# A fixed order for the opening of a hybrid decoder step: small rows, constants and key norms moved

## The chip, the cores and the metric

The kernel runs on one core of a Trainium2 chip. The metric is the device time of one execution in microseconds (us): the median of several runs. Before the change it is 1969.95 us (three runs, 1969.76 to 1970.19).

The engines of a core run side by side, each through its own list of instructions in order, and wait for one another by semaphores: TensorE (PE: matrix products and transposes, into PSUM banks), VectorE (DVE), ScalarE (ACT), GpSimd (POOL), and SyncE (SP), which here only issues transfers (DMA).

## The reference, cut to what matters

One layer of a decoder, on a prompt of 2048 tokens and on 8 samples of one token each. All of it is float32, D_MODEL is 1024.

```python
mod = (c @ w_ada + b_ada)[:, None, :]
shift, scale, gate = jnp.split(mod, 3, axis=-1)
h = _rmsnorm(x, norm_g) * (1.0 + scale) + shift
z = h @ w_in
q, k, v, ga, xr, gr, ma, mr = jnp.split(z, offs, axis=-1)
q = _rmsnorm(q.reshape(B, T, N_HEADS, HEAD_DIM), q_g)
k = _rmsnorm(k.reshape(B, T, KV_HEADS, HEAD_DIM), k_g)
o = _band_attention(q, k, v, rel_table, sinks)      # window of 128, bias by distance
ya = o * jax.nn.silu(ga)
xc, conv_new = _causal_conv(xr, conv_buf, w_conv, b_conv)
hs, h_last = _rglru(xc, h0, w_ra, b_ra, w_rx, b_rx, lam)
yr = hs * jax.nn.silu(gr)
merged = jax.nn.sigmoid(ma) * (ya @ w_pa) + jax.nn.sigmoid(mr) * (yr @ w_pr)
y = x + gate * (merged @ w_out)
```

In the recurrent branch (_rglru) the decay is exp(-8 r softplus(-lam)) with r = sigmoid(x @ w_ra + b_ra). The constants of that branch are softplus(-lam) for each of the 1024 channels, worked out by a series, and half the biases of the two gates.

## The kernel before

The prompt is done in two halves of 1024 rows (s = 0, 1). A float32 product is made of three products of rounded parts: each operand is split into a high part (a cast on ACT) and a low part (source minus high, on DVE), and PE adds high x high, high x low and low x high. A weight's step thus waits first for ACT's cast and, at its third matmul, for DVE's split.

**The opening** (s = 0) is the loop over f = 0 to 9 near line 2053. Turn f loads w_ada columns, multiplies them by the vector c on PE (col_tiled, L295, whose result ACT copies to a tile H), transposes that tile on PE and reduces it on DVE (mod_finish, L310) to shift and scale of 128 channels (modT, gsT). PE turns a column block of the first four normed x tiles (x_turn), and ACT, then DVE, evacuate it as scaled high and low parts (h_evac, L376). Between these stand the matmuls of the first four tiles of keys and values (kv_part), two turns behind. rms_rows (x_rms) norms an x tile: squares on ACT, the power on POOL, the products on DVE. In turns 7 to 9 the other four x tiles are turned (second). This part is recorded with `pinned[0] = True`: the scheduler keeps the order in which it is written. Into it are set: in turn 4 the loads of the rows of small vectors (vrows_rest, nine transfers of 0.2 to 16 KB), in turns 5 and 6 the two steps of the table of biases (bias_table: a transpose, a copy on DVE, a matmul, a store to Ed), in turn 7 the loads from Ed.

**Then, not pinned,** come the transposes of the small rows to VT, the stores of h (late, sixteen of them), the constants of the recurrent branch (ba2, c4: two activations and 25 operations on 128 x 8 elements, L2107 to L2124), the states of the samples (rows, turned by eight small transposes on PE to RT), and the stage of keys and values (phase_kv, L502). There k_tile (L449) norms a tile's keys in two steps: the first takes the squares (ACT), sums them (DVE), takes the power (POOL) and multiplies (DVE), the second turns the keys on PE and evacuates them; v_tile copies the values and subtracts the tile before. The scheduler may mix these with the matmuls of the next tiles (half). phase_attn (L554) is a generator: at its first step it issues the first loads of weights, at the second it splits some.

PSUM's eight banks are shared: tag g has three, q two, t three. In the opening the first three key tiles hold the banks of g and the fourth one bank of t, so that turns, column sums, transposes and the table of biases go through two banks of t.

**After the attention** a list of steps runs (class Line): step t is twelve matmuls on PE, and then the events of step t in the order EVAC, SIDE, SPLIT, FORM, CHAIN, LATE, STORE, LOAD. The weights of a step are loaded seven steps and split two steps ahead. gate_side (SIDE, steps 10 to 39) makes the gate's columns.

Of the kernel before, what the change touches and what calls it, by code (L numbers as in the profile page):

```python
# [16 lines left out]
ALU = mybir.AluOpType  # L17
# [24 lines left out]
def tile_hybrid_step(ctx: ExitStack, tc: tile.TileContext, x_prompt, x_sample, cache_k, cache_v, state_conv,  # L42
# [63 lines left out]
    def H(shape, dt=F32):  # L106
        return hp.tile([P] + shape, dt, tag="H", name=nm("H"))
# [341 lines left out]
    def k_tile(s, tt, ps, kT):  # L449

        ss = head_rstd(ps, P)
        kn = H([4, HD])
        V.tensor_tensor(kn, ps[:, :256].rearrange("p (h d) -> p h d", d=HD),
                        ss.unsqueeze(2).broadcast_to([P, 4, HD]), op=ALU.mult)
        yield
        p2 = PT()
        for Gp in range(2):
            T_.transpose(p2[:, Gp * P:(Gp + 1) * P], kn[:, 2 * Gp:2 * Gp + 2, :].rearrange("p h d -> p (h d)"), ident)
        for Gp in range(2):
            src = p2[:, Gp * P:(Gp + 1) * P]  # L460
# [41 lines left out]
    def phase_kv(s, hT, sa, kT, vt, wk, wv, start, tts, side, attn):  # L502


        def half(ps, tt, h):
            for j, w in enumerate((wk, wv)):
                for k in range(4 * h, 4 * h + 4):
                    wh, wl, _ = w[k]
                    xh, xl = col(hT, k, tt * P, P)
                    o = ps[:, j * 256:(j + 1) * 256]  # L510
                    T_.matmul(o, xh, wh, start=(j == 0 and k == 0), stop=False, skip_group_check=True)
                    T_.matmul(o, xh, wl, start=False, stop=False, skip_group_check=True)
                    T_.matmul(o, xl, wh, start=False, stop=(k == KT - 1), skip_group_check=True)

        pend = []

        def evac(ps, tt):
            pend.append(k_tile(s, tt, ps, kT))
            next(pend[-1])
            v_tile(s, tt, ps[:, 256:512], vt)  # L520

        def flush(n):
            while len(pend) > n:
                next(pend.pop(0))

        next(attn)
        for tt, ps in start:
            evac(ps, tt)
        for tt in tts[:-2]:
            ps = PQ()  # L530
            half(ps, tt, 0)
            flush(1)
            half(ps, tt, 1)
            evac(ps, tt)
            next(side, None)
            next(side, None)
        if s == 1:
            kv_samples(wk, wv, sa)
        two = [(tt, PG()) for tt in tts[-2:]]
        for tt, ps in two:  # L540
            half(ps, tt, 0)
            flush(0)
            next(side, None)
        drop(wk[0:4] + wv[0:4])
        next(attn)
        for tt, ps in two:
            half(ps, tt, 1)
            evac(ps, tt)
        drop(wk[4:8] + wv[4:8])
        for _ in side:  # L550
            pass
        return pend

    def phase_attn(s, hT, sa, kT, vt, chunks, line):  # L554
# [257 lines left out]
        pinned[0] = True  # L812
# [440 lines left out]
    def stages(s, hT, hT1=None, side=None):  # L1253
# [603 lines left out]
    def reload_h(line, hT, k, c, t):  # L1857
# [11 lines left out]

        line.on(t - 3, LOAD, load)  # L1870
        line.on(t, FORM, split)

    def gate_side():

# [178 lines left out]
    for f in range(KT + 2):  # L2053
# [38 lines left out]
    ba2 = C([P, 16], tag="ba2")  # L2092
    V.tensor_scalar(ba2, VT[:, 72:88], 0.5, None, op0=ALU.mult)


    sk = M([NH])
    ld.dma_start(sk, sinks[0].partition_broadcast(P))
# [5 lines left out]

    kT, vt = kv_tiles()
    wk, wv = wkv[0][0] + wkv[1][0], wkv[0][1] + wkv[1][1]

    lam = VT[:, 88:96]  # L2107
    e8, s8, q8, r8 = (M([8]) for _ in range(4))
    A.activation(e8, lam, AF.Abs)
    A.activation(e8, e8, AF.Exp, scale=-1.0)  # L2110
    V.tensor_scalar(s8, e8, 2.0, None, op0=ALU.add)
    V.reciprocal(s8, s8)
    V.tensor_tensor(s8, s8, e8, op=ALU.mult)
    V.tensor_tensor(q8, s8, s8, op=ALU.mult)
    V.tensor_scalar(r8, q8, 1.0 / 17, 1.0 / 15, op0=ALU.mult, op1=ALU.add)
    for n in (13, 11, 9, 7, 5, 3, 1):
        V.tensor_tensor(r8, r8, q8, op=ALU.mult)
        V.tensor_scalar(r8, r8, 1.0 / n, None, op0=ALU.add)
    V.tensor_tensor(r8, r8, s8, op=ALU.mult)
    V.tensor_scalar(s8, lam, -1.0, 0.0, op0=ALU.mult, op1=ALU.max)  # L2120
    c4 = C([P, 16], tag="c4")
    V.scalar_tensor_tensor(c4[:, 0:8], r8, 2.0, s8, op0=ALU.mult, op1=ALU.add)
    V.tensor_scalar(c4[:, 0:8], c4[:, 0:8], 4.0, None, op0=ALU.mult)
    V.tensor_scalar(c4[:, 8:16], c4[:, 0:8], -1.0, None, op0=ALU.mult)  # L2124


    rows = S([D])
    ld.dma_start(rows[0:24], state_conv[0].rearrange("b r d -> (b r) d"))
    ld.dma_start(rows[24:32], state_h[0])
    ps = PT()  # L2130
    for k in range(KT):
        T_.transpose(ps[:, k * 32:(k + 1) * 32], rows[0:32, k * P:(k + 1) * P], ident[0:32, 0:32])
    RT = C([P, KT, 32], tag="RT")
    V.tensor_copy(RT, ps[:, 0:256].rearrange("p (k c) -> p k c", c=32))
    free(rows)
# [8 lines left out]
    line = stages(1, hT1)  # L2144
    kT, vt = kv_tiles()
    attn = phase_attn(1, hT1, side["sa"], kT, vt, chunks, line)
    pend = phase_kv(1, hT1, side["sa"], kT, vt, side["k"], side["v"], [], range(8), iter(()), attn)
    attn.send(pend)
    line.run()
# [28 lines left out]
```

## Time and profile before

| what | value |
|---|---|
| median of three runs | 1969.95 us |
| the profiled execution | 1970.57 us |
| its span, first to last instruction | 1968.9 us |
| mean granted clock of PE | 0.996 |
| PE busy | 1918.9 us, 97% |
| DMA | 286.61 MB, 146 GB/s |

A profile's timeline gives start, duration, engine, line, operation, the tile written and the tiles read, and in brackets how long the engine had been idle and what ended that. All tiles go through one helper, so that every line is L60, and operations are told apart by their tiles: S, B, H and M are SBUF tiles (rings of 28 and 35, and pools of 6 and 16), pg, pq and pt are PSUM banks of tags g, q and t. A window's row gives its bounds, its length, an engine's busy time, PE's granted clock (1.00 is full speed), the DMA engines' busy share and GB/s.

### The profile page before, as it was taken

The numbers are of one execution on the slowest core, as the hardware profiler recorded it, in microseconds if no ns is written. First come the engines' busy times: TensorE is split into PE (matmuls) and PEld (weight loads), VectorE is DVE, ScalarE is ACT, GpSimd is POOL, SyncE is SP. The second block draws the span as 40 slices with busy tenths as digits, with TensorE's granted clock in tenths as the row PEclk, the third lists the DMA queues.
The fourth block names the chain that finished last, engine by engine and source line by source line (L and its number), as shares of the span: only waits on it lengthen the run. The fifth ranks groups of instructions, "written<-read, shape, count | busy, mean of one in ns | idle before, by whom it ended". The sixth has DMA issues, their size and how long they took to land. (4 is left out here: it accounts for less than half of the span.)

```text
span 1968.9 us, 32371 instructions
## 1 busy us (share of the span) xinstructions
PE 1918.9 (97%) x11504; PEld 1569.0 (80%) x11504; DVE 1376.8 (70%) x2862; ACT 985.0 (50%) x2167; POOL 391.3 (20%) x476
## 2 busy tenths in 40 slices
PE   6899999999999999999999999999999999999999
PEld 4798986778888878877898888777887887777777
DVE  3557778567887876587735776776677879755965
ACT  4435665336575766323424555543475667532321
POOL 2213443000111113150022333300010201111600
PEclk9899999999999999999999999999999999999999
DMA  9521125652433567976611111544233325458673
GB/s 280 175 65 51 48 77 158 202 171 93 138 118 100 176 190 251 330 243 191 228 47 49 55 34 51 160 124 151 82 119 108 126 93 167 144 170 300 214 236 108
DMA packets 307686, 286.61 MB, mean 146 GB/s; under 512 B 57073, under 2 KB 224229, under 8 KB 307486
## 3 DMA queue, kind: packets, MB, share of 16 engines
q1 hardware_dynamic: 307398, 282.41, 45.8%
q0 software_dynamic: 128, 2.15, 0.3%
q8 instruction: 90, 1.47, 0.3%
q14 instruction: 70, 0.57, 0.1%
HBM read 200.69 MB, written 85.93 MB: 146 GB/s over the span
## 5 line engine op out<-in xcount | busy, mean ns | idle before, releaser
L60 PE MATMUL pg<-S,B 128*128 128x512 f32 (+1 forms) x4224 | 1003.7, 392 | 4.2 <-DVE B L60 3.8
L60 PEld LDWEIGHTS pg<-S,B 128*128 128x128 f32 (+1 forms) x4224 | 773.9, 188 | 188.6 <-issue 11.1
L60 DVE TENSOR_TENSOR B<-B,B 128x512 fp32r<-128x512 f32 (+1 forms) x732 | 540.9, 761 | 145.8 <-ACT B L60 136.0
L60 PE MATMUL pq<-S,B 128*128 128x512 f32 (+2 forms) x1920 | 412.2, 379 | 6.7 <-DVE B L60 6.6
L60 PEld LDWEIGHTS pq<-S,B 128*128 128x128 f32 (+1 forms) x1920 | 317.0, 188 | 85.2 <-DVE B L60 10.6
L60 POOL TENSOR_TENSOR B<-B,B 128x512 f32<-128x512 f32 x128 | 191.4, 1513 | 921.5 <-DVE B L60 363.5
L60 ACT CAST B<-B 128x512 fp32r<-128x512 f32 x468 | 279.9, 617 | 111.4 <-DVE B L60 71.5
L60 PE MATMUL pg<-B,S 128*128 128x256 f32 x1872 | 243.3, 286 | 0.0
L60 PEld LDWEIGHTS pg<-B,S 128*128 128x128 f32 x1872 | 228.1, 189 | 10.1 <-issue 9.4
L60 DVE TENSOR_TENSOR S<-B,S 128x512 fp32r<-128x512 f32 x184 | 144.6, 814 | 25.9 <-ACT S L60 25.7
L60 ACT CAST S<-B 128x512 fp32r<-128x512 f32 x184 | 109.3, 620 | 94.0 <-DVE B L60 40.7
L60 ACT ACTIVATE B<-B 128x512 f32<-128x512 f32 (+1 forms) x150 | 93.1, 629 | 117.0 <-DVE B L60 109.0
L60 ACT ACTIVATE B<-B,M 128x129 f32<-128x129 f32 x260 | 102.6, 396 | 91.3 <-DVE M L60 87.1
L60 DVE SCALAR_TENSOR_TENSOR B<-B,pg 128x512 f32<-128x512 f32 x78 | 53.1, 682 | 72.9 <-PE pg L60 63.1
L60 ACT COPY H<-pt 128x256 f32<-128x256 f32 (+1 forms) x55 | 18.5, 337 | 160.9 <-PE pt L60 160.9
L60 DVE TENSOR_TENSOR B<-pq,B 128x512 f32<-128x512 f32 x96 | 65.9, 686 | 44.3 <-PE pq L60 38.3
L60 POOL TENSOR_TENSOR B<-B,M 128x512 f32<-128x512 f32 x64 | 68.6, 1093 | 122.8 <-DVE M L60 122.8
L60 ACT COPY B<-pg 128x512 f32<-128x512 f32 x80 | 46.8, 586 | 89.4 <-PE pg L60 81.1
L60 ACT ACTIVATE B<-pg 128x512 f32<-128x512 f32 x76 | 45.2, 595 | 85.3 <-PE pg L60 85.3
L60 POOL TENSOR_TENSOR M<-M,mhalf 128x8 f32<-128x8 f32 (+4 forms) x70 | 83.8, 1198 | 5.8
L60 DVE SCALAR_TENSOR_TENSOR B<-B,VT,B 128x512 f32<-128x512 f32 x96 | 81.2, 846 | 2.3
L60 DVE TENSOR_TENSOR B<-pt,mcT 128x512 f32<-128x512 f32 x64 | 41.7, 686 | 47.4 <-ACT B L60 45.5
(201 smaller groups left out, 1718.6 us busy)
## 6 DMA issues: line engine op xcount, KB each, us to landing
B<-in_w_in_dram SPq DMA_DIRECT2D x144, 256.0 KB
B<-in_w_in_dram SPq DMA_DIRECT2D x128, 128.0 KB
B<-yad SPq DMA_DIRECT2D x56, 256.0 KB
B<-hd SPq DMA_DIRECT2D x48, 256.0 KB
B<-in_w_out_dram SPq DMA_DIRECT2D x48, 256.0 KB
S<-in_w_ada_dram SPq DMA_DIRECT2D x32, 256.0 KB
S<-in_x_prompt_dram SPq DMA_DIRECT2D x16, 512.0 KB
hd<-B SPq DMA_DIRECT2D x32, 256.0 KB
```

The source lines that it names most:

```text
L60: ins = fn(*args, **kw)
```

## The change

All of the opening and of the attention's first part is now recorded in the written order; the pieces that were left to the scheduler are put in places:

- The table of biases goes from turns 5 and 6 to turns 2 and 3; the loads of small rows go from turn 4 to turn 6, behind all loads of w_ada.
- The first eight stores of h are issued in turn 8, the other eight behind the first loads of the attention's weights.
- ba2, c4 and RT are made by a generator rnn_side in steps 16 (loads), 22 (constants) and 24 (transposes) of the list of steps of half 0.
- k_tile yields once more, between the power and the product, and evac takes several tiles: the first four are normed in two pairs, all later ones singly, with the values' copy and subtraction ahead of the product.

```diff
     def k_tile(s, tt, ps, kT):
 
         ss = head_rstd(ps, P)
+        yield
         kn = H([4, HD])
...
-        def evac(ps, tt):
-            pend.append(k_tile(s, tt, ps, kT))
-            next(pend[-1])
-            v_tile(s, tt, ps[:, 256:512], vt)
+        def evac(*tiles):
+            gens = [k_tile(s, tt, ps, kT) for tt, ps in tiles]
+            for g in gens:
+                next(g)
+            for tt, ps in tiles:
+                v_tile(s, tt, ps[:, 256:512], vt)
+            for g in gens:
+                next(g)
+            pend.extend(gens)
...
-        next(attn)
-        for tt, ps in start:
-            evac(ps, tt)
+        for n in range(0, len(start), 2):
+            evac(*start[n:n + 2])
...
         prefetch(3)
-        pinned[0] = s == 1
-        yield
-        pinned[0] = True
+        yield
         weights(-1, 0)
-        pinned[0] = s == 1
         pend = yield
-        pinned[0] = True
         weights(-1, 1)
...
             line.steps(gate_side(), range(10, 40), SIDE)
+            line.steps(rnn_side(), (16, 22, 24), SIDE)
...
+    def rnn_side():
+
+        rows = [Tt([512]) for _ in range(2)]
+        for h, r in enumerate(rows):
+            ld.dma_start(r[0:24], state_conv[0].rearrange("b r d -> (b r) d")[:, h * 512:(h + 1) * 512])
+            ld.dma_start(r[24:32], state_h[0][:, h * 512:(h + 1) * 512])
+        yield
+        V.tensor_scalar(ba2, VT[:, 72:88], 0.5, None, op0=ALU.mult)
...
+        yield
+        ps = PT()
+        for k in range(KT):
+            T_.transpose(ps[:, k * 32:(k + 1) * 32], rows[k // 4][0:32, k % 4 * P:(k % 4 + 1) * P], ident[0:32, 0:32])
+        V.tensor_copy(RT, ps[:, 0:256].rearrange("p (k c) -> p k c", c=32))
+        free(*rows)
+        yield
...
-        if f == 4:
+        if f in (2, 3):
+            next(table)
+        if f == 6:
             next(rest)
-        if f in (5, 6):
-            next(table)
         if f == 7:
             bias_load()
...
-    pinned[0] = False
+        if f == KT:
+            for fn in late[:KT]:
+                fn()
     next(rest)
-    for fn in late:
-        fn()
...
+    next(attn)
+    for fn in late[KT:]:
+        fn()
     pend = phase_kv(0, hT, None, kT, vt, wk, wv, list(enumerate(kvp)), range(4, 8), bias_expand(), attn)
```

Three places of the changed order. First DVE in the opening, where turn 2 passes into turn 3 (S_239 and S_242 are x tile 4 being normed, pt_481 and pt_488 the transposed column sums of turn 3). Before:

```order
L60 TENSOR_TENSOR B_424<-B_186,B_423 128x512
L60 TENSOR_SCALAR S_239<-S_239,M_439 128x512 x2
L60 TENSOR_REDUCE modT_118<-pt_481 128x9
L60 TENSOR_SCALAR modT_118<-modT_118,VT_105 128x9
L60 TENSOR_REDUCE modT_118<-pt_481 128x9
```

With the change (pt_452 is the turned table, H_454 its copy, pt_514 and H_516 the second step):

```order
L60 TENSOR_TENSOR B_427<-B_189,B_426 128x512
L60 TENSOR_SCALAR S_242<-S_242,M_442 128x512 x2
L60 COPY H_454<-pt_452 32x128
L60 TENSOR_REDUCE modT_118<-pt_488 128x9
L60 TENSOR_SCALAR modT_118<-modT_118,VT_105 128x9
L60 TENSOR_REDUCE modT_118<-pt_488 128x9
L60 TENSOR_SCALAR modT_118<-modT_118,VT_105 128x9
L60 TENSOR_SCALAR gsT_154<-modT_118,VT_105 128x9
L60 TENSOR_TENSOR S_496<-B_498,S_496 128x512
L60 TENSOR_SCALAR H_516<-pt_514 16x128 x2
```

The copy of the table, which in the order before stood behind the norming of x tiles 6 and 7, now stands behind that of x tile 4 and ahead of turn 3's reductions; pt_452 and pt_488 are the same PSUM bank.

Second PE at the start of the stage of keys and values (pt_998 are the samples' states being turned; H_1033, H_1042, H_1052 and H_1062 are the normed keys of tiles 0 to 3; pq_1150 is tile 5, its matmuls are cut to one for each run). Before, the pieces at the first and the last tile:

```order
L60 MATMUL pq_1150<-B_419,S_414 128x256
L60 MATMUL pt_998<-ident_81,S_995 128x32 x8
L60 MATMUL pt_1091<-ident_81,H_1033 128x128 x2
L60 MATMUL pq_1150<-B_420,S_414 128x256
```

```order
L60 MATMUL pq_1150<-B_555,S_638 128x256
L60 MATMUL pt_1147<-S_810,B_154 128x512
L60 MATMUL pt_1175<-ident_81,H_1062 128x128 x2
L60 MATMUL pq_1150<-B_556,S_638 128x256
L60 MATMUL pq_1150<-B_555,S_638 128x256
```

With the change (H_998, H_1000 and H_1018 are the keys of tiles 0 to 2, pq_1022 is tile 4):

```order
L60 MATMUL pq_1022<-B_427,S_497 128x256
L60 MATMUL pq_1022<-B_426,S_497 128x256
L60 MATMUL pt_1047<-ident_81,H_998 128x128 x2
L60 MATMUL pt_1054<-ident_81,H_1000 128x128 x2
L60 MATMUL pt_1061<-ident_81,H_1018 128x128 x2
L60 MATMUL pq_1022<-B_568,S_563 128x256
L60 MATMUL pq_1022<-B_569,S_563 128x256
```

Before, 55 matmuls of tiles 4 and 5 stand ahead of the keys of tile 0, and five to twenty between one tile's keys and the next; now 24 stand ahead, and the keys of three tiles follow one another. pt_1061 has the bank of the fourth key tile's matmuls.

Third DVE at step 22 of the list of steps (B_4801 and B_4828 are gates, B_4874 is the low half of the weights of step 24, B_4895 that of step 25, M_4844 and M_4846 the series). With the change:

```order
L60 SCALAR_TENSOR_TENSOR B_4801<-B_4801,B_4739 128x512
L60 TENSOR_SCALAR ba_31_151<-VT_105 128x16
L60 TENSOR_SCALAR M_4844<-M_4843 128x8
L60 RECIPROCAL M_4844<-M_4844 128x8
L60 TENSOR_TENSOR M_4844<-M_4844,M_4843 128x8
L60 TENSOR_TENSOR M_4845<-M_4844 128x8
L60 TENSOR_SCALAR M_4846<-M_4845 128x8
L60 TENSOR_TENSOR M_4846<-M_4846,M_4845 128x8
```

```order
L60 TENSOR_SCALAR c_32_152<-c_32_152 128x8 x2
L60 TENSOR_TENSOR B_4874<-B_4691,B_4873 128x512
L60 TENSOR_TENSOR B_4801<-B_4801,B_4802 128x512
L60 SCALAR_TENSOR_TENSOR B_4828<-B_4828,B_4772 128x512
L60 TENSOR_TENSOR B_4895<-B_4721,B_4894 128x512
```

Before, the row of B_4874's split followed that of the gate B_4801 at once; now the 25 operations of the constants stand between them.

More of the change, by code (lines that the diff above doesn't have):

```diff
@@ L533, in phase_kv @@
             half(ps, tt, 1)
-            evac(ps, tt)
+            evac((tt, ps))
             next(side, None)
@@ L547, in phase_kv @@
             half(ps, tt, 1)
-            evac(ps, tt)
+            evac((tt, ps))
         drop(wk[4:8] + wv[4:8])
@@ L803, in phase_attn @@
         smp = [stage_s(u) for u in range(4)]
-        pinned[0] = True
         prefetch(3)
-        pinned[0] = s == 1
         yield
-        pinned[0] = True
         weights(-1, 0)
-        pinned[0] = s == 1
         pend = yield
-        pinned[0] = True
         weights(-1, 1)
@@ L1871, in reload_h @@
         line.on(t, FORM, split)
+    ba2, c4 = (C([P, 16], tag=t) for t in ("ba2", "c4"))
+    RT = C([P, KT, 32], tag="RT")
+    def rnn_side():
[5 more added lines that the diff above has]
+        V.tensor_scalar(ba2, VT[:, 72:88], 0.5, None, op0=ALU.mult)
+        lam = VT[:, 88:96]
+        e8, s8, q8, r8 = (M([8]) for _ in range(4))
+        A.activation(e8, lam, AF.Abs)
+        A.activation(e8, e8, AF.Exp, scale=-1.0)
+        V.tensor_scalar(s8, e8, 2.0, None, op0=ALU.add)
+        V.reciprocal(s8, s8)
+        V.tensor_tensor(s8, s8, e8, op=ALU.mult)
+        V.tensor_tensor(q8, s8, s8, op=ALU.mult)
+        V.tensor_scalar(r8, q8, 1.0 / 17, 1.0 / 15, op0=ALU.mult, op1=ALU.add)
+        for n in (13, 11, 9, 7, 5, 3, 1):
+            V.tensor_tensor(r8, r8, q8, op=ALU.mult)
+            V.tensor_scalar(r8, r8, 1.0 / n, None, op0=ALU.add)
+        V.tensor_tensor(r8, r8, s8, op=ALU.mult)
+        V.tensor_scalar(s8, lam, -1.0, 0.0, op0=ALU.mult, op1=ALU.max)
+        V.scalar_tensor_tensor(c4[:, 0:8], r8, 2.0, s8, op0=ALU.mult, op1=ALU.add)
+        V.tensor_scalar(c4[:, 0:8], c4[:, 0:8], 4.0, None, op0=ALU.mult)
+        V.tensor_scalar(c4[:, 8:16], c4[:, 0:8], -1.0, None, op0=ALU.mult)
+        yield
[5 more added lines that the diff above has]
+        yield
     def gate_side():
@@ L2085, in tile_hybrid_step @@
             second(i)
-    pinned[0] = False
+        if f == KT:
+            for fn in late[:KT]:
+                fn()
     next(rest)
-    for fn in late:
-        fn()
     qg = C([P, 1], tag="qg")
     V.tensor_scalar(qg, VT[:, 96:97], -(HD ** -0.5), None, op0=ALU.mult)
-    ba2 = C([P, 16], tag="ba2")
-    V.tensor_scalar(ba2, VT[:, 72:88], 0.5, None, op0=ALU.mult)
     sk = M([NH])
@@ L2105, in tile_hybrid_step @@
     wk, wv = wkv[0][0] + wkv[1][0], wkv[0][1] + wkv[1][1]
[L2107 to L2135, printed above, removed]
     hT1, side = [], {}
@@ L2146, in tile_hybrid_step @@
     attn = phase_attn(1, hT1, side["sa"], kT, vt, chunks, line)
+    next(attn)
     pend = phase_kv(1, hT1, side["sa"], kT, vt, side["k"], side["v"], [], range(8), iter(()), attn)
```

## The prediction

> **What bounds the kernel now.** I read the page first, then TensorE's waits, then stretches with the granted clock, then the timeline of the places that the change touches.
>
> ```profile
> PE 1918.9 (97%) x11504; PEld 1569.0 (80%) x11504; DVE 1376.8 (70%) x2862; ACT 985.0 (50%) x2167; POOL 391.3 (20%) x476
> PE pt L60 <- DVE RT L60: 3.1, 1, 3.1
> 50.30:53.50 3.20, 0.01 (x1) 1.00 0.98 278
> 53.50:56.90 3.40, 3.36 (x16) 0.50 1.06 399
> 80.00:83.10 3.10, 0.00 (x0) 1.00 0.78 178
> 83.10:84.20 1.10, 1.07 (x9) 1.00 0.00 0
> 84.20:91.10 6.90, 6.27 (x25) 0.51 0.00 0
> 91.10:98.10 7.00, 7.00 (x49) 1.00 0.18 75
> ```
>
> TensorE is the bound: 97% busy, so the time can only fall where it idles or runs at half clock, and anything that stops it later in the program is paid in full. In the stretches the columns are length, busy time, clock, DMA share and GB/s. Two holes of the opening count: 3.2 us at 50.3, then 3.4 us at clock 0.50; 3.1 us at 80.0, then 6.9 us at 0.51. Those are what the change can reach.
>
> **The change, part one: the table of biases two turns earlier.** In the loop over f the chain of one turn is: ACT copies the columns' sums (H), PE transposes them, DVE reduces them, ACT scales the tile, then ACT copies the next H. Turn 6 ends so:
>
> ```profile
> 50.79 0.35 ACT L60 COPY H<-pt 128x256 f32<-128x256 f32 x1
> 52.33 0.88 DVE L60 TENSOR_SCALAR S<-S,M 128x512 f32<-128x512 f32 x2 [0.71 <-POOL M L60]
> 53.13 0.27 DVE L60 COPY H<-pt 32x128 f32<-32x128 f32 x1
> 53.54 0.66 PE L60 MATMUL pt<-ident,H 128*128 128x128 f32 x2 [3.24 <-DVE H L60]
> 54.24 0.20 DVE L60 TENSOR_REDUCE modT<-pt 128x9 f32<-128x36 f32 x1 [0.84 <-PE pt L60]
> 58.25 0.37 ACT L60 COPY H<-pt 128x256 f32<-128x256 f32 x1 [0.49 <-PE pt L60]
> 60.04 0.38 PE L60 MATMUL pt<-ident,H 128*128 128x128 f32 x2
> 61.51 0.78 ACT L60 ACTIVATE B<-pq,modT,gsT 128x512 f32<-128x512 f32 x1 [2.89 <-DVE gsT L60]
> ```
>
> The table's copy on DVE (53.13) stands behind the norming of the last x tile (52.33), and PE's transposes need the PSUM bank that it reads: 3.24 us. The change sets the same copy behind the norming of x tile 4, in front of turn 3's reductions, and the next transposes again need its bank. So the wait moves:
>
> ```profile
> 31.09 1.67 PE L60 MATMUL pg<-B,S 128*128 128x256 f32 x12
> 33.20 0.35 ACT L60 COPY H<-pt 128x256 f32<-128x256 f32 x1
> 33.61 0.44 PE L60 MATMUL pt<-ident,H 128*128 128x128 f32 x2 [0.84 <-ACT H L60]
> 34.51 0.88 DVE L60 TENSOR_SCALAR S<-S,M 128x512 f32<-128x512 f32 x2 [1.71 <-POOL M L60]
> 35.31 0.19 DVE L60 TENSOR_REDUCE modT<-pt 128x9 f32<-128x36 f32 x1
> 38.33 0.38 PE L60 MATMUL pt<-ident,H 128*128 128x128 f32 x2
> 56.69 0.49 PE L60 MATMUL pt<-H,rel 32*16 32x128 f32 x2
> ```
>
> DVE reaches the copy at 35.31 instead of the reduction; PE follows 0.41 later (53.13 to 53.54), at 35.7 instead of 33.6: +2.1. PE is busy from there to turn 4's transposes (38.33) and now has the table's matmul too (56.69, 0.4), so those come at 40.8: +2.5. I carry +2.5 through the chain, since each turn waits for the one before on ACT. Turn 6: H copied at 50.79 + 2.5 = 53.3, transposes at 53.7 without the bank wait; but the norming of x tile 7 ends at 52.33 + 0.88 + 2.5 = 55.7, and the reduction comes then: +1.5 on 54.24. Turn 7: ACT's copy was ready at 58.25 - 0.49, now 59.2; PE, no longer at half clock, transposes 0.4 later, 59.6 instead of 60.04; ACT's evacuation follows 1.47 behind (60.04 to 61.51): 61.1. **Term A: -0.4**, where the removed wait alone would have promised 3. Bounds: -2.9 if turn 3 did not wait, +1 if DVE's other work lies in the way.
>
> The rows of small vectors, the nine tiny loads, go behind the last loads of w_ada. I cost this at nothing: PE waits for none of the loads behind them. What covers it is the same chain on ACT; without it the last w_ada tile, issued some us earlier, could be worth part of a wait. SP's other moves, the first weights ahead of the second eight stores of hd and the sinks behind the first eight, I cost at nothing too: no wait of PE names these transfers. If the sinks came late, DVE would stand in front of the first reduction of part two, and C would grow by as much.
>
> **The idle clock.** PE will sit from the end of the matmuls before (31.09 + 1.67 = 32.76) to 35.7: 2.95 us. A hole of 3.1 us, followed by 1.1 us of work, dropped the clock at 84.2; the other drop came right behind 3.2 us. The switches of the trace (53.5, 56.9, 84.2, 91.1) lie on a grid of 3.41 us; carried back it has a window from 33.0 to 36.4, in which PE would work 0.7 us, less than the 1.1 us that did not keep the clock. So I take a drop: 3.4 us at half clock, in a stretch where PE sets turn 4. **Term F: +1.7**, else 0. The Trainium skill, "TensorE: Matmul & The Clock Gate", section "Why this matters for your kernels", asks only for no PE-idle gaps above about 3 us; this gap is just under, and by that rule the sum would be 1.7 less. The trace's rows at 80.0 to 84.2 speak for a window that need not be wholly idle; no row has a gap just like this one.
>
> **Part two: the norms of the keys.** Rows of before:
>
> ```profile
> 71.89 6.53 PE L60 MATMUL pq<-B,S 128*128 128x256 f32 x53
> 73.77 0.69 DVE L60 TENSOR_TENSOR S<-B,S 128x512 fp32r<-128x512 f32 x1 [0.50 <-ACT S L60]
> 75.30 0.41 DVE L60 TENSOR_REDUCE M<-H 128x4 f32<-128x256 f32 x1
> 76.08 1.02 POOL L60 TENSOR_TENSOR M<-M,mhalf 128x4 f32<-128x4 f32 x1
> 77.14 0.42 DVE L60 TENSOR_TENSOR H<-pg,M 128x256 f32<-128x256 f32 x1 [1.11 <-POOL M L60]
> 78.36 0.68 PE L60 MATMUL pt<-ident,S 32*128 32x32 f32 x8
> 97.64 1.02 PE L60 MATMUL pt<-S,B 128*128 128x512 f32 x2
> 98.10 11.96 PE L60 MATMUL pg<-B,S 128*128 128x256 f32 x96
> ```
>
> One square and two tiny activations leave ACT's last evacuations (an estimate of -0.4, from 0.35 for a copy of as many columns), so with A the last split on DVE starts at 73.77 - 0.8 = 73.0. Behind it: the split 0.6, three small operations of 0.2, so the first reduction at 74.2 (75.30 before, the constants stood in its way), power at +0.78, product at +1.06, transposes at +0.41: 76.45. The second tile is one power and its scaling later (1.3): 77.75. The second pair's reductions stand behind both products, so its products come at 77.34 + 0.34 + 0.78 + 1.06 = 79.5 and 80.8. The third tile's transposes need the bank that the fourth tile's product frees: 81.2.
>
> What fills PE until then? Before, the scheduler let 53 matmuls run (71.89) and the hole came at 80. In the fixed order PE has 24 of them: from 71.1, 24/53 of 6.53 us, to 74.05. Then it stands, but for 0.4 us of transposes, for 6.7 us, against 3.1 (RT, which goes) and some 0.6. From 81.4 there are 96 matmuls of 0.123 (11.8), four of the bias at 0.46 (97.64 to 98.10), three pairs of transposes at 0.22: 14.3 at full clock. Half clock after such a hole lasted 3.4 and 6.9 us; I take 5.1, a loss of 2.55. The long run that began at 98.10 begins at 98.25. **Term C with A: +0.2**, bounds -0.9 and +1.6 by the half clock's two lengths and some 0.7 for slack at half clock.
>
> **Part three: constants in the recurrent stage.** 25 small operations on DVE, each needing the one before, and two on ACT go to step 22 of the line of stages:
>
> ```profile
> 74.82 0.17 DVE L60 TENSOR_TENSOR M<-M,M 128x8 f32<-128x8 f32 x1
> 75.02 0.17 DVE L60 TENSOR_TENSOR M<-M 128x8 f32<-128x8 f32 x1
> 382.54 5.84 PE L60 MATMUL pg<-S,B 128*128 128x512 f32 x24
> 383.97 0.61 ACT L60 CAST B<-B 128x512 fp32r<-128x512 f32 x1
> 384.78 0.68 DVE L60 SCALAR_TENSOR_TENSOR B<-B,B 128x512 f32<-128x512 f32 x1
> 385.38 1.29 DVE L60 TENSOR_TENSOR B<-B,B 128x512 fp32r<-128x512 f32 x2
> 388.22 5.76 PE L60 MATMUL pq<-S,B 128*128 128x512 f32 x24
> ```
>
> Steps 22 and 23 are the matmuls at 382.54, step 24 begins at 388.22. Its weights' low half is the split at 385.38, and the constants now stand ahead of it: 25 x 0.2 us (the spacing of 74.82 and 75.02) = 5.0. The split starts at 390.4 and is done at 391.05. Step 24 does two matmuls with the high half (ACT's cast waits only for two tiny operations), to 388.7, and stands until 391.05. **Term D: +2.4**; bounds 1.6 (0.17 apart, the duration itself) and 3.6 (0.25). Behind the split stand a product, the next silu and the split of step 25, done by 393.0, when PE is still in step 24: no second wait. The 2.3 us hole may drop the clock too (term G, +1.7, not in the forecast). **Term E:** the eight small transposes, 0.6 of PE (78.36), already taken out of C, now stand between steps 24 and 25: +0.6, bounds 0.3 and 0.7. Four row loads on SP, with seven steps of lead behind them: nothing; if the lead were gone, a load's 2 us. The second half's keys keep their ACT order and only swap a subtraction ahead of a product on DVE; no PE wait of before names them: nothing.
>
> **Sum.** +0.2 (A, C) + 1.7 (F) + 2.4 (D) + 0.6 (E) = +4.9. The profiled execution took 1970.57 us, span 1968.9; with the change 1975.5. The median shown is 1969.95, 0.6 below, so I predict 1974.8. About 0.2%, 3.9 us, is what a measurement of this kernel can tell from no change.
>
> **Rivals.**
> 1. The clock holds at turn 3, since the grid falls otherwise or the gap is too short: 1974.8 - 1.7 = 1973.1, within 0.2%. For it: no row has a 2.95 us gap. Chance 0.28. The rule of the Trainium skill cited above would have it so.
> 2. The clock drops in step 24's hole as well: 1974.8 + 1.7 = 1976.5. For it: a window of 3.41 us there would be a third busy, as the one before 84.2 was. Chance 0.16.
> 3. Not slower: turn 3's transposes do not wait, the opening keeps what the words promise. The price is A: -2.9 instead of -0.4, and no F: 1974.8 - 2.5 - 1.7 = 1970.6. It decides at the bank that those transposes get; the order of waits in the changed program speaks against it. Chance 0.12.
> 4. The change does more than I see, in the pairs above all (both reductions behind one wait), and DVE's chain of constants fits in its idle time: below 1966.0. Against it: the split of step 24 is due 2.4 us earlier than it can come. Chance 0.07.
>
> **Numbers.** Forecast 0.37, rivals 0.28, 0.16, 0.12, 0.07. Slower by over 0.2%: 0.37 + 0.16 + a little of rival 1 (bounds of C) = 0.57. Within: 0.36. Faster: 0.07. The range reaches to rival 3 at 1970.6 and, above, past rival 2 by C's bound: 1978.0; outside it lie rival 4 and the far ends.
>
> **What would show it.** A: PE's transposes of turn 3 waiting about 2 us for DVE's copy, none of 3.2 us at turn 6, ACT's evacuation of turn 7 near 61. F: clock 0.5 for some 3.4 us from about 36. C: PE with two or three holes between 74 and 81.5, the long run of matmuls beginning near 98 to 100. D: one wait of PE for DVE of 2 to 3 us near 390, behind a row of tiny DVE operations. I am wrong if turn 3 shows no wait, or if step 24 starts on time.

## The result, and the profile after

| | kernel before | changed kernel |
|---|---|---|
| median of the runs | 1969.86 us (1969.42 to 1970.19, 4 runs) | 1979.79 us (1976.99 to 1981.97, 4 runs) |
| ratio to before [95% interval] | | 1.0051 [1.0037, 1.0065] |
| profiled execution, its span | 1970.57 us, 1968.9 us | 1981.16 us, 1979.2 us |

The change makes the kernel slower by 9.9 us, half a per cent. Forecast were 4.9 us and at most 1978.0: the sign was right, the size was not. The changed kernel's runs lie 5 us apart, those of the kernel before 0.8. Of the runs of the experiments below, one of experiment 14 (2342 us) and one of the kernel before beside it (2095 us) had a far lower granted clock (0.75 and 0.85), and the ratios leave them out.

First the line of engines on the page of the changed kernel: TensorE is busy 3.1 us longer with the same 11504 matmuls, and the span grew by 10.3, so TensorE also stands 7.2 us longer.

```profile
PE 1922.0 (97%) x11504; PEld 1570.6 (79%) x11504; DVE 1375.9 (70%) x2862; ACT 984.1 (50%) x2167; POOL 392.2 (20%) x476
```

TensorE's waits (total, times, longest). The waits for RT (3.1) are gone; those for H that DVE ended rose from 3.2 in one to 8.9 in four, those that ACT ended from 0.8 in one to 4.1 in three, those for the weights B from 6.6 to 9.4.

```profile
PE pq L60 <- DVE B L60: 9.4, 8, 2.5
PE pt L60 <- DVE H L60: 8.9, 4, 3.1
```

TensorE's timeline at the places of the prediction (start, length, the wait ahead and who ended it):

```profile
36.20 0.41 PE L60 MATMUL pt<-ident,H 128*128 128x128 f32 x2 [2.86 <-DVE H L60]
...
55.57 0.44 PE L60 MATMUL pt<-ident,H 128*128 128x128 f32 x2 [2.36 <-ACT H L60]
...
61.34 0.44 PE L60 MATMUL pt<-ident,H 128*128 128x128 f32 x2 [0.90 <-ACT H L60]
...
73.11 3.09 PE L60 MATMUL pq<-B,S 128*128 128x256 f32 x24
78.55 0.66 PE L60 MATMUL pt<-ident,H 128*128 128x128 f32 x2 [2.35 <-DVE H L60]
79.83 0.69 PE L60 MATMUL pt<-ident,H 128*128 128x128 f32 x2 [0.62 <-DVE H L60]
83.59 0.66 PE L60 MATMUL pt<-ident,H 128*128 128x128 f32 x2 [3.07 <-DVE H L60]
...
101.24 11.96 PE L60 MATMUL pg<-B,S 128*128 128x256 f32 x96
...
391.39 0.63 PE L60 MATMUL pq<-S,B 128*128 128x512 f32 x2
394.55 3.44 PE L60 MATMUL pq<-S,B 128*128 128x512 f32 x10 [2.52 <-DVE B L60]
397.92 1.06 PE L60 MATMUL pt<-ident,B 32*128 32x32 f32 x8
...
403.66 1.07 PE L60 MATMUL pt<-B,cT 128*32 128x256 f32 x16
```

The last of these operations, before:

```profile
393.91 1.07 PE L60 MATMUL pt<-B,cT 128*32 128x256 f32 x16
```

Read from above: turn 3 waits for the table's copy; turn 6 no longer waits for DVE, but TensorE still stands 2.36 us there, until ACT has copied H (3.24 before); turn 7's transposes come at 61.34 (60.04 before); in the keys' stage 24 matmuls end at 76.2 and three waits follow; the long run of 96 matmuls begins at 101.24 (98.10 before); step 24 begins at 391.39 (388.22 before) and stands 2.52 us for its low half; the matmuls that came at 393.91 before come at 403.66.

Then stretches of 3.41 us (length, TensorE's busy time, granted clock, DMA share, GB/s), cut where the clock changes:

```profile
34.16:37.57 3.41, 1.37 (x12) 1.00 0.95 319
37.57:40.98 3.41, 3.41 (x24) 0.50 1.15 320
...
75.12:78.53 3.41, 1.08 (x10) 1.00 1.04 396
78.53:81.94 3.41, 1.35 (x4) 0.50 0.10 40
81.94:85.36 3.42, 1.77 (x9) 0.50 0.00 0
85.36:88.77 3.41, 3.41 (x18) 0.50 0.02 5
...
392.56:395.97 3.41, 1.42 (x6) 1.00 0.01 4
395.97:399.38 3.41, 3.41 (x14) 0.50 0.57 196
399.38:402.80 3.42, 3.42 (x9) 0.50 1.01 295
```

The holes of the timeline, but for the one at turn 6, are followed by half clock: 3.4 us behind turn 3, 10.2 in the keys' stage, 6.8 behind step 24. At step 24 TensorE is busy all of the 6.8 us, so 3.4 us are lost on top of the wait. The cause of the wait stands in VectorE's timeline: the 25 constants begin at 388.57, and the split that step 24 waits for comes behind the last.

```profile
388.57 0.17 DVE L60 TENSOR_SCALAR ba<-VT 128x16 f32<-128x16 f32 x1
...
393.17 0.38 DVE L60 TENSOR_SCALAR c<-c 128x8 f32<-128x8 f32 x2
393.80 1.29 DVE L60 TENSOR_TENSOR B<-B,B 128x512 fp32r<-128x512 f32 x2 [0.26 <-issue]
```

### The profile page after: what moved, and what is told of

Its sections match the earlier page's. It is cut to its first block, busy times and chain, and to the rows that moved or that the text cites. A ratio compares the mean times of both kernels' runs of the same rounds, so it can differ in the third digit from the quotient of the medians.

```text
span 1979.2 us, 32383 instructions
## 1 busy us (share of the span) xinstructions
PE 1922.0 (97%) x11504; PEld 1570.6 (79%) x11504; DVE 1375.9 (70%) x2862; ACT 984.1 (50%) x2167; POOL 392.2 (20%) x476
```

## The experiments

Fourteen kernels ran, thirteen edits of the changed one and itself again. They ran in four groups (1 to 4, 5 to 8, 9 to 11 and 12 to 14), each on a chip of its own and with the kernel before beside it. The median varies by chip and by the clock's luck (the kernel before had 1968.7 to 1970.8 in the four groups), so the ratio to the kernel before on the same chip is given too.

**1. The constants in six portions** (lines of `rnn_side`; the four temporaries become tiles of their own, as they now live longer).

```diff
         V.tensor_tensor(s8, s8, e8, op=ALU.mult)
+        yield
...
         for n in (13, 11, 9, 7, 5, 3, 1):
             V.tensor_tensor(r8, r8, q8, op=ALU.mult)
             V.tensor_scalar(r8, r8, 1.0 / n, None, op0=ALU.add)
+            if n in (13, 9, 5, 1):
+                yield
-            line.steps(rnn_side(), (16, 22, 24), SIDE)
+            line.steps(rnn_side(), (16, 17, 18, 19, 20, 21, 22, 24), SIDE)
```

> The constants' 25 DVE operations are cut into six portions, at steps 17 to 22, four or five operations (0.8 to 1.0 us) each, instead of all at step 22. Theory: what the changed kernel lost at step 24 is the wait for the late split (2.5 us) and the half clock behind it (6.8 us long, 3.4 lost). No portion is long enough to make a split late, so both go: 1979.8 - 5.9 = 1973.9, and the trace has no wait of PE and no clock of 0.5 between 380 and 405. Rival 1: the clock falls somewhere near in any case, since its windows run free of the program: only the wait goes, 1977.3. Rival 2: DVE has no room between steps 17 and 22 either, and the portions make other splits late: 1979 or more, with several short waits of PE there.

Measured: 1972.07 us (12 runs), ratio 1.0015 [1.0005, 1.0026]. TensorE's timeline of this kernel shows step 24 in one piece, with no wait:

```profile
385.17 5.83 PE L60 MATMUL pg<-S,B 128*128 128x512 f32 x24
390.83 2.96 PE L60 MATMUL pq<-S,B 128*128 128x512 f32 x12
```

and its clock is 1.00 from 88 to 1128 us. So the theory holds, rivals 1 and 2 fall: DVE has room for the 5 us, only not in one piece. The gain against the changed kernel (1979.5 in experiment 5) is 7.4 us, 1.5 more than expected.

**2. A filler in the hole** (ten matmuls whose result nobody reads, behind step 23).

```diff
+            def warm():
+                ps, x = PT(), F["x11"][0][:, 0, :]
+                for n in range(10):
+                    T_.matmul(ps, x[:, 0:P], x, start=(n == 0), stop=(n == 9))
+            line.on(23, LATE, warm)
```

> The changed kernel, with ten matmuls of 128x512 whose result nobody reads added on PE ahead of step 24's (an estimate of 2.4 us: 24 matmuls took 5.76), where PE stood 2.5 us. They only fill the hole: the split of step 24 comes as late as before. Theory: the hole drops the clock, and that costs 3.4 us more than the wait; with PE busy the clock holds: 1979.8 - 3.4 = 1976.4, no 0.5 in the clock between 390 and 405, and PE's wait for the split under 0.5. Rival 1: the clock's fall has another cause than this hole: 1979.8, and 0.5 in the clock there as before. Rival 2: the added work is no filler but in the way (PE reaches step 24 later than the split): above 1980.

Measured: 1973.76 us (12 runs), ratio 1.0030 [1.0020, 1.0041]. TensorE's timeline at that place:

```profile
390.38 2.43 PE L60 MATMUL pt<-S 128*128 128x512 f32 x10
...
393.53 2.58 PE L60 MATMUL pq<-S,B 128*128 128x512 f32 x10 [0.25 <-DVE B L60]
```

The split is as late as before, TensorE does useless work instead of standing, and the kernel is 5.7 us faster than the changed one by the medians, 4 to 5 by the ratios (1.0051 and 1.0056 to 1.0030). Expected were 3.4, which the intervals of the ratios leave room for. In the first profile of the changed kernel the half clock at this place cost 3.4 us, more than the wait of 2.5 that brought it on.

**3. Norms one by one.**

```diff
-        for n in range(0, len(start), 2):
-            evac(*start[n:n + 2])
+        for n in range(len(start)):
+            evac(start[n])
```

> The changed kernel, with the norms of the first four key tiles one by one instead of in pairs. Theory: the pairs help, and the opening's loss comes from the fixed order, which leaves PE 24 matmuls to fill the time of the norms. One by one each reduction stands behind the product of the tile before it, so the four products follow at 2.3 us instead of 1.4, 2.3 and 1.4: the third tile's transposes come some 2 us later than 83.6, and the time is 1979.8 + 2 = 1981.8. Rival: the pairs lost the opening's 1.8 us of the keys' stage, since both reductions stand ahead of the first product: 1979.8 - 1.8 = 1978.0, with the third tile's transposes before 83.

Measured: 1979.06 us (6 runs), 1.0048 [1.0032, 1.0063]: the medians show no difference from the changed kernel. The trace does: TensorE waits 2.12, 1.82 and 3.92 us for the keys (2.35, 0.62 and 3.07 in pairs), and from turn 7's transposes to the long run it takes 101.79 - 60.40 = 41.4 us, where the four profiles with pairs (the first, experiments 1, 2 and 5) have 38.9 to 39.9, mean 39.3. So the pairs gain some 2 us in the trace, as the theory had it and against the rival; the half clock in this stage also differs between these profiles (10.2 us here and in the first, 6.8 in the other three), and against the first alone the difference is 1.5. This run also shows the hole at step 24, here 2.16 us, without half clock behind it (stretches of this kernel):

```profile
393.03:396.44 3.41, 1.77 (x8) 1.00 0.11 43
396.44:399.85 3.41, 3.41 (x21) 1.00 0.54 171
```

**4. The table back at turns 5 and 6.**

```diff
-        if f in (2, 3):
+        if f in (5, 6):
             next(table)
```

> The changed kernel, with the table of biases back at turns 5 and 6. Theory: the wait of 2.9 us and the half clock leave turn 3, and the wait of 3.2 us with its half clock comes back at turn 6, so turn 7's transposes come at 60.0 instead of 61.3: 1979.8 - 1.3 = 1978.5. Rival 1: turn 3's half clock was the only loss, and turn 6 does not wait in this fixed order: turn 7's transposes before 58, 1975.5 to 1976.5. Rival 2: turn 6 waits and the rest of the opening is limited by something behind it (the norms of the keys), which takes the gain back: 1979.8.

Measured: 1979.42 us (6 runs), 1.0052 [1.0036, 1.0068]: no difference. TensorE's row at turn 6 has the old wait back, with the half clock at 43 and 57 instead of 37:

```profile
55.65 0.41 PE L60 MATMUL pt<-ident,H 128*128 128x128 f32 x2 [3.39 <-DVE H L60]
```

Turn 7's transposes come at 62.16 and the long run at 103.37, later than in any profile of the changed opening (60.5 to 61.4, 99.6 to 101.2). So by the trace the theory and rival 1 fall: moving the wait from turn 6 to turn 3 was no loss. The time is nearest to rival 2's, though its mechanism isn't seen; with runs from 1976.9 to 1983.5 the median alone could not tell it from the theory's 1978.5.

**5. The changed kernel again**, no edit.

> The changed kernel once more, with nothing edited, so that the others of this batch have it on their own chip, and for the spread of its runs. Theory: the clock is decided in windows of 3.413 us that begin at a random point of the program, a window less than half busy is followed by one at half clock, and a hole of 2.5 us at step 24 leaves such a window in about 2.5 / 3.41 = 0.7 of the runs. So its runs fall in two heaps some 3.4 us apart, the higher ones at a granted clock lower by 0.0017 (3.4 / 1979), median 1978 to 1980. Rival: the half clock at step 24 belongs to the program: one heap.

Measured: 1979.50 us (1976.03 to 1981.81, 5 runs), 1.0056 [1.0044, 1.0069]. With the first four runs there are nine: 1976.0, 1977.0, 1978.4, 1978.9, 1979.5, 1980.5, 1981.2, 1981.8, 1982.0 at clocks 0.993 to 0.996. That is a spread, but not two heaps; the half clock comes and goes at more than one place. The profiled run, the fastest, had one stretch of half clock at step 24 where the first profile had two:

```profile
389.89:393.30 3.41, 0.90 (x4) 1.00 0.15 48
393.30:396.71 3.41, 3.41 (x9) 0.50 0.40 148
```

Its long run began at 99.57 (101.24 in the first profile; 100.54 and 100.25 in experiments 1 and 2, whose opening is the same).

Turn 6 is one of these places. Of the ten profiles with the table's copy where the change sets it (the first and experiments 1, 2, 3, 5, 6, 9, 11, 13 and 14), nine have the hole of 2.36 us there and the tenth one of 1.56; in six of them half clock follows. In experiment 1:

```profile
56.49:59.90 3.41, 3.41 (x25) 0.50 0.95 293
```

**6. The fill** (`phase_kv`: 48 matmuls of tile 4 ahead of the first keys).

```diff
             half(ps, tt, 0)
-            flush(1)
+            if len(pend) < 3:
+                flush(1)
             half(ps, tt, 1)
+            flush(2)
             evac((tt, ps))
```

> The changed kernel, with PE's matmuls of key tile 4 (48) and of tile 5 (48) set ahead of the transposes of key tiles 0 and 1, and of tile 2, where 24 stood ahead of all three. Theory: the keys' stage lost its time because PE had too little to do while the norms ran; its holes of 2.35, 0.62 and 3.07 us and the half clock behind them (some 3 us) go: 1979.8 - 8 = 1971.8, with no wait of PE for H over 1 us between 73 and 100 and no 0.5 in the clock there. Rival 1: the stage is bound by the chain of norms itself, and something behind it (the squares of tiles 4 and 5, the first scores) waits in its place: 1976 to 1980. Rival 2: only the half clock goes, since the holes move: 1976.8.

Measured: 1974.73 us (5 runs), 1.0036 [1.0022, 1.0049]. TensorE's timeline:

```profile
73.01 5.96 PE L60 MATMUL pq<-B,S 128*128 128x256 f32 x48
...
79.73 0.44 PE L60 MATMUL pt<-ident,H 128*128 128x128 f32 x2 [0.54 <-DVE H L60]
83.46 1.10 PE L60 MATMUL pt<-S,B 128*128 128x512 f32 x2 [3.28 <-issue]
```

The wait of 2.35 is gone, but the third hole came back at another instruction, the first matmul of the expanded bias: between theory (1971.8) and rival 2 (1976.8).

**7. The table's copy ahead of the norming of x tile 4.**

```diff
+        if f in (2, 3):
+            next(table)
         for i in {2: (4,), 4: (5,), 5: (6, 7)}.get(f, ()):
             x_rms(i)
-        if f in (2, 3):
-            next(table)
```

> The changed kernel, with the table's copy ahead of the norming of x tile 4 on DVE instead of behind it. Theory: turn 3's transposes no longer wait for DVE: they come at ACT's copy of H (33.68 + 0.35 + 0.1 = 34.1) instead of 36.2, but the reductions still stand behind the norming, so the chain gains only 36.65 - 35.86 = 0.8; the hole falls to some 1 us, so no window there is half idle, and the half clock (1.7 lost) goes too: 1979.8 - 2.5 = 1977.3. Rival 1: the chain gains the whole 2.1 and the half clock: 1976.0. Rival 2: turn 6 or the keys' norms take it back: 1979.8, with turn 7's transposes at 61.3 as before.

Measured: 1974.84 us (5 runs), 1.0033 [1.0020, 1.0046]. TensorE at turns 3 and 7:

```profile
33.78 0.44 PE L60 MATMUL pt<-ident,H 128*128 128x128 f32 x2 [0.74 <-ACT H L60]
...
57.70 0.44 PE L60 MATMUL pt<-ident,H 128*128 128x128 f32 x2 [0.88 <-ACT H L60]
```

Neither turn 3 nor turn 6 waits for DVE, no half clock lies there, and turn 7 comes 3.6 us earlier than in the changed kernel, 2.3 earlier than before. Expected were 2.5 us; measured 4.7. Two lines, set the one way or the other round, decide whether this part of the change gains.

**8. Edits 1, 6 and 7 together.**

> Three edits at once: the constants in six portions, the fill of 48 matmuls, the table's copy ahead of the norming. Theory: the three places are apart (33 to 37, 73 to 90, 390 us) and add up: 1979.8 - 6.5 (as measured for the portions alone) - 8 - 2.5 = 1962.8, faster than the kernel before (ratio about 0.9965). Rival 1: the first two share the half clock of the opening, and the gain of one is partly that of the other: 1965 to 1968. Rival 2: the fill gives nothing: 1970.8.

Measured: 1969.10 us (11 runs), 1.0003 [0.9994, 1.0012]. The theory misses by 6 us, nearest is rival 1. The hole of 3.28 us ahead of the bias is there as in 6, and so is the half clock behind it.

**9. The fill with a later bias**: as 6, and the first two pieces of the bias wait until tile 5's first 24 matmuls are issued.

```diff
+            elif tt == 5:
+                next(side, None)
+                next(side, None)
             half(ps, tt, 1)
...
-            next(side, None)
-            next(side, None)
+            if tt != 4:
+                next(side, None)
+                next(side, None)
```

> The fill once more, with the first piece of the expanded bias (the matmuls S by B into pt) set behind tile 5's first 24 matmuls instead of ahead of them. The fill alone still had one hole of 3.28 us ahead of just that matmul, with a clock of 0.5 for 3.4 us behind it. Theory: this matmul takes the PSUM bank of key tile 3, which is free only when that tile's product is done on DVE (79.6 + 0.4 in the run of all three edits), so what stood behind it waited; with 24 matmuls (3.1 us) ahead of it the hole is under 0.7 and the clock holds: 1974.7 - 2.6 - 1.7 = 1970.4. Rival: the bank is not the reason, and the hole moves to the next matmul of the bias or to the next transposes: 1974.7.

Measured: 1972.13 us (11 runs), 1.0006 [0.9997, 1.0015]. The bias now waits 0.45 us and the long run begins at 94.91 (98.98 in 6). The hole did not move on, so the rival falls. That the PSUM bank of key tile 3 was the reason fits all four profiles with the fill: this matmul starts 0.1 us after DVE's product of that tile ends (83.35 to 83.46 in 6, 80.03 to 80.14 in 8, 83.50 to 83.60 here, 79.83 to 79.94 in 10).

**10. Edits 1, 7 and 9 together.**

> The portions, the table's copy ahead of the norming, and the fill with the late bias, together. Theory: 1969.1 (the three edits before) - 4.3 (2.6 of hole, 1.7 of clock) = 1964.8, faster than the kernel before by 0.2%. Rival 1: the half clock there came in some runs only: 1966.0. Rival 2: as for the fill with the late bias alone, the hole only moves: 1969.1.

Measured: 1966.27 us (6 runs), 0.9971 [0.9958, 0.9983]. Faster than the kernel before, and nearest to rival 1; the long run begins at 91.22.

**11. The order of the keys' stage left to the scheduler.**

```diff
+    pinned[0] = False
     next(rest)
...
+        pinned[0] = True
         prefetch(3)
+        pinned[0] = s == 1
         yield
```

(and the same pair around the next two steps of `phase_attn`, as in the kernel before)

> The changed kernel, with the order of the keys' stage left to the scheduler as in the kernel before, all else as changed. Theory: the fixed order costs the keys' stage its filling, since the scheduler sets 22 matmuls of tile 4 between the keys of the first and the third tile and more behind: a part of the fill's gain, 1979.5 - 2.5 = 1977.0, the waits of PE for H between 73 and 90 together under 4 us instead of 6. Rival: the scheduler has no more to put there than the fixed order, as the norms are the bound: 1979.5.

Measured: 1969.87 us (11 runs), 0.9992 [0.9983, 1.0001]. Both expectations are far off: this part of the change alone is worth 9.6 us by the medians, and 12.6 by the ratios (1.0056 to 0.9992). VectorE and TensorE of this kernel:

```profile
70.21 0.42 DVE L60 TENSOR_REDUCE M<-H 128x4 f32<-128x256 f32 x1 [0.26 <-ACT H L60]
...
73.34 0.41 DVE L60 TENSOR_TENSOR H<-pg,M 128x256 f32<-128x256 f32 x1
```

```profile
75.55 0.60 PE L60 MATMUL pt<-ident,H 128*128 128x128 f32 x4
...
79.76 0.41 PE L60 MATMUL pt<-ident,H 128*128 128x128 f32 x2 [1.46 <-DVE H L60]
...
92.94 11.94 PE L60 MATMUL pg<-B,S 128*128 128x256 f32 x96
```

and the same two operations of VectorE in the changed kernel:

```profile
76.00 0.74 DVE L60 TENSOR_REDUCE M<-H 128x4 f32<-128x256 f32 x2
...
77.98 0.42 DVE L60 TENSOR_TENSOR H<-pg,M 128x256 f32<-128x256 f32 x1 [0.91 <-POOL M L60]
```

The scheduler sets the first reduction between the splits of x, 5.8 us earlier, and the first product 4.6 us earlier; the fixed order sets them behind the last split. The hole in all is 1.46 us instead of 6.04, and the long run begins 8.3 us earlier than in the changed kernel, 5.2 earlier than before. This profile drew no half clock in the opening, where the first profile of the changed kernel lost 6.8 us to it and that of the kernel before 5.1, so these two differences are in good part the clock's.

**12. Free order and edits 1 and 7.**

> The keys' stage left to the scheduler, the constants in six portions, the table's copy ahead of the norming of x tile 4. Theory: the three losses lie in three places (36, 73 to 90 and 390 us) and add up: 1969.9 (scheduler alone) - 6.5 (portions) - 2 (table) = 1961.4, faster than the kernel before, ratio about 0.995. Rival: what the scheduler's run gained came partly from windows of the clock that fell well, and the sum is that of the best of the fixed orders, 1966.

Measured: 1960.50 us (1960.40 to 1961.92, 5 runs), 0.9954 [0.9941, 0.9968]: the fastest of all, and where the theory had it. The long run begins at 89.77, the profile has no half clock before the program's end, and its page has

```profile
PE 1911.3 (98%) x11504; PEld 1562.6 (80%) x11504; DVE 1376.9 (70%) x2862; ACT 983.3 (50%) x2167; POOL 394.1 (20%) x476
```

TensorE is busy 10.7 us less than in the changed kernel with the same matmuls, since none of them runs at half clock. Its five runs lie within 1.5 us, all at a mean granted clock of 1.000. A part of that is luck, as the rival has it: this kernel still has holes of 1.50 and 0.79 us, 0.6 apart, near 1114 us, and in nine of the sixteen profiles half clock follows this pair. Over all sixteen, the half clock behind 500 us loses 1.9 us on the average, so an estimate without the luck is 1962.4, still the lowest.

**13 and 14. Which engine's order it was.** In 13 TensorE's order in the keys' stage is free and the others' fixed, in 14 the reverse (same places as in 11; the condition in `call` names the engine).

> The changed kernel, with PE's order in the keys' stage left to the scheduler and DVE's, ACT's, POOL's and SP's fixed as in the change. PE then has 42 matmuls ahead of the keys of tile 0 and 1, where 24 stood. Theory A (PE's filling is what the fixed order took): nearly the whole of the 9.6 us that the free stage gained: 1970. Theory B (the fixed order of DVE and ACT sets the first norms behind the last splits of x, some 2.5 us later than the scheduler does, and this is what the stage loses): the first two holes are filled, the third tile's wait stays at about 2 us with its half clock: 1979.5 - 4.5 = 1975.

> The other way round: PE's order fixed as in the change, DVE's, ACT's, POOL's and SP's left to the scheduler, which sets the squares and reductions of key tiles 0 and 1 between the last casts and splits of x. Theory A: without the filling nothing is gained: 1979.5. Theory B: the keys of tiles 0 and 1 are ready when PE has done its 24 matmuls, the third tile's come near 80 instead of 83.6 and one hole of some 3 us is left: 1979.5 - 5.5 = 1974.

Measured: 13 has 1972.05 us (11 runs), 1.0010 [1.0001, 1.0019]; 14 has 1973.63 us, 1.0013 [1.0004, 1.0023]. TensorE of 13:

```profile
77.84 0.41 PE L60 MATMUL pt<-ident,H 128*128 128x128 f32 x2 [1.05 <-DVE H L60]
79.12 0.69 PE L60 MATMUL pt<-ident,H 128*128 128x128 f32 x2 [0.76 <-DVE H L60]
```

and of 14:

```profile
75.45 0.60 PE L60 MATMUL pt<-ident,H 128*128 128x128 f32 x4
79.33 0.66 PE L60 MATMUL pt<-ident,H 128*128 128x128 f32 x2 [3.28 <-DVE H L60]
```

With TensorE alone free the keys are as late as in the changed kernel, but TensorE has 35 matmuls to do first (not the 42 of the expectation); with the other engines free the keys of tiles 0 and 1 are there when the 24 matmuls end, and one hole is left. Each half gives most of the gain (7.4 and 5.9 us by the medians, 9.1 and 8.5 by the ratios), both give 9.6 (12.6): the holes add up to 1.8 us in 13, 3.3 in 14, 1.5 with both free and 6.0 with both fixed. The late products and the empty queue of TensorE do most of their harm together, so neither theory holds alone; by size A is nearer for 13 and B for 14.

## Why the prediction was wrong

| term | predicted | in the profiled execution |
|---|---|---|
| A and F, to turn 7's transposes | -0.4 + 1.7 = +1.3 | 61.34 - 60.04 = +1.3 |
| C, from there to the long run | 0.2 + 0.4 = +0.6 | (101.24 - 98.10) - 1.3 = +1.8 |
| D, the wait at step 24 | +2.4 | +2.5 |
| G, half clock behind it | 0 (1.7 in a rival) | 6.83 / 2 = +3.4 |
| E, the eight transposes | +0.6 | 403.66 - 393.91 - 3.14 - 2.52 - 3.41 = +0.7 |
| the rest of the program | 0 | (1979.20 - 1968.86) - 9.75 = +0.6 |

- **A was right** in size, and in the wait for DVE: it moved from turn 6 to turn 3 (2.86 there, 2.1 and 2.95 had been worked out for delay and hole), and putting it back gains nothing (experiment 4). Two things I didn't see. One place further up on DVE there is no wait at all (experiment 7). And turn 6 keeps a hole of 2.36 us, since ACT copies H only at 55.17, behind its squares for x tiles 6 and 7; it doesn't delay turn 7, whose chain waits for the norming of x tile 7 (the reduction comes at 57.50), but half clock follows it in six of ten profiles, and the sum had no term for that.
- **D and E were right** to 0.1 us, and portions take D away (experiment 1).
- **The step that failed is G**: "The 2.3 us hole may drop the clock too (term G, +1.7, not in the forecast)". F, of the same kind and with nearly the same hole, stood in the forecast as certain; G was put at nothing there, and the rival that held it got a chance of 0.16 and one window of half clock. Over the ten profiles that have the hole at step 24, seven have the half clock behind it, and four of these for 6.8 us, not 3.4. Their mean loss is (4 x 3.4 + 3 x 1.7) / 10 = 1.9 us; in the first profile it is 3.4. With the filler, which takes away this half clock alone, the kernel is 5.1 us slower than the one before by the medians (experiment 2; the ratio 1.0030 makes it 5.9), close to the 4.9 that the sum has without G.
- **F was drawn as certain, too.** It came in seven of the ten profiles whose turn 3 waits as in the change. The window "from 33.0 to 36.4" was carried over from the grid of the kernel before's run, and the grid lies elsewhere in each run; that F came in the profiled execution, and the first row of the table with it, is luck of about seven in ten.
- **C was nearly right on the average and too small in the profiled run**: 10.2 us of half clock, where 5.1 had been taken. Over the four profiles with this opening the long run began at 99.6 to 101.2, mean 100.4; the sum had 100.0. But its reason was incomplete. It said of the first reduction "75.30 before, the constants stood in its way": with the constants gone and the order free it comes at 70.21, and it was the fixed order that held it at 76.0. So in experiment 11's profile the rest of the change gained 5.2 us in the opening (98.10 to 92.94), with no half clock there, and the fixed order gave 8.3 back; 6.8 of these are half clock that one profile drew and the other didn't. I had counted what the fixed order costs in matmuls of TensorE alone, 24 for 53.
- **What stays open**: by the mean granted clock of all runs (0.9940 in nine runs of the changed kernel, 0.9960 in eighty of the kernel before) some 0.0020 x 1977 = 4 us of the 9.9 are half clock; the profiles name 1.9 of it at step 24 and some in the opening. Where the rest lies isn't shown, since most runs have no profile.

The small rows, sinks and stores on SP, costed at nothing, have not been tried apart.

## What to carry to other kernels

In these traces a hole on TensorE costs its length, and from some 1.7 us on, with a chance that grows with it (seven in ten at 2.2 to 2.5 us), another 1.7 to 3.4 us by half clock: keep holes short, or fill them with any work. Small serial work must go into a stage in portions no longer than the slack of the next operation that TensorE waits for, not in one block at a free-looking step. And fixing an order by hand fixes every engine's: before pinning what a scheduler did, look at what it had interleaved on each of them, here the reductions between the splits.

## What the runs showed of the hardware

The clock of TensorE in these traces is decided in windows. In sixteen profiles every stretch at 0.5, but for the one cut off by the program's end, is 3.413, 6.827 or 10.240 us long, and within a run they start on one grid of 3.413 us that lies differently in each run. Count TensorE's busy share of each window of the grid at full clock (from 25 us after the start to 14 us before the end): of 45 windows that were busy less than 0.45, all are followed by half clock; of some 8900 that were busy half of it or more, one is; of 13 in between, six. The hole of 2.2 to 2.5 us at step 24 shows both sides: busy 1.42 of 3.41 in the first profile of the changed kernel, then 0.50; 1.77 in experiment 3, then 1.00. At half clock the way back asks for more: 13 of 13 windows busy less than 0.86 are followed by another at half clock, and 4 of 56 busier ones. So a hole alone between full work halves the clock where more than some 1.7 us of it fall into one window, which by estimate, for one of 2.2 to 2.5 us, is 2.2 / 3.41 = 0.6 to 2.5 / 3.41 = 0.7 of the positions of the grid; seven of ten were seen.

The Trainium skill, "TensorE: Matmul & The Clock Gate", section "What's actually happening", has the same window: 3413 ns and free-running, not reset when a kernel starts. The traces agree. The section "Why this matters for your kernels", by which F would not have come, asks for no gaps above about 3 us; here gaps of 2.2 to 2.5 us at step 24 were followed by half clock in seven of ten profiles, and those of 2.6 to 2.9 us at turn 3 in seven of ten, so the measured share of the window decides.
